# Queries and keys projected with the weights stationary and 512 tokens moving, keys turned back for their output, the decode's first cache fetches behind the queries' stores

## The chip, the cores and the metric

The kernel runs on one core of one Trainium2 chip. The metric is the device time of one execution in microseconds (us); the median of the runs shown is what two kernels are compared by. TensorE (PE) multiplies, and has a row of its own for weight loads (PEld); VectorE (DVE), ScalarE (ACT) and GpSimd (POOL) do the element-wise work; SyncE (SP) issues nearly all DMAs, on one queue. The granted clock of TensorE was 0.995 of full in the profiled execution.

## The reference

One layer of a streaming encoder runs on 1024 prompt tokens, and on 8 x 16 new tokens that are decoded against caches. RMSNorm is followed by one projection to queries, keys and values of two head groups. Group A (8 heads of 64) does stick-breaking attention over all the past; group B (8 heads) does softmax attention over a band of chunks. Then come per-head norms, an output projection, a gated feed-forward block and an input embedding.

```python
def trunk_layer(x, p, g_mix, w_in, ...):
    h = rmsnorm(x, g_mix)
    q_a, k_a, v_a, q_b, k_b, v_b = split_heads(h, w_in)      # h @ w_in, cut into six parts of 512 columns
    a = stick_breaking(q_a, k_a, v_a, ...)                   # prompt: causal; decode: the cache and the new frames
    o_b = chunk_band_prompt(q_b, k_b, v_b, rel_table)        # decode: band_attention over the cached band
    x = x + concat(rmsnorm(a), rmsnorm(o_b)) @ w_out
    x = x + (silu(rmsnorm(x) @ w_gate) * (rmsnorm(x) @ w_up)) @ w_down
    return x + sigmoid(rmsnorm(x) @ w_ple_gate) * (p @ w_ple_proj), (k_a, v_a, k_b, v_b)
```

The keys and values of the prompt (all rows of group A, the last 512 rows of group B) and of the decoded tokens are outputs too.

## The kernel before, in words

**Tokens and precision.** The 1024 prompt tokens and the 128 decoded ones make nine tiles of 128 tokens; the ninth is the decoded one. A product of float32 values is made of three matmuls of high and low parts (`mm3`, lines 105 to 108: high by high on line 106, and the two mixed ones on 107 and 108). The normalised activations are turned so that the contracted dimension lies on the partitions, and stay in SBUF as `hT`, in three groups of three token tiles (384 tokens, class `Transposed`).

**The projection.** `qkv` (line 217) is a generator which yields after each unit of TensorE work. It goes through twelve column groups of 256 columns of `w_in`, in the order of `loads` (line 289): keys of A (two groups), queries of A (two), values of A (two, interleaved), keys of B, values of B, queries of B. A column group's weights come by one DMA of 1 MB (`wraw`, a single buffer), and are split into high and low parts by ACT and POOL (lines 150 and 111).
- Keys and values (`others`, line 248): per token tile, 24 matmuls (8 slices of the contraction by 3) with the tokens as the stationary operand (lhsT) and 256 weight columns moving. The result `ps` holds tokens on partitions. ACT or DVE copies it to `st` (line 257), which is stored as the output (lines 278 and 284). Keys are also turned by TensorE (line 263, six transposes for three tiles), split into high and low parts (`parts`, lines 223 and 111) and stored to a DRAM scratch, `kT0h`, `kT0l` (group A) or `kT1h`, `kT1l` (group B).
- Queries (`queries`, line 234): per 128 columns and 384 tokens, 24 matmuls with the weights stationary and 384 tokens moving. The result is already turned; ACT and DVE scale and split it (lines 226 and 227) and it is stored to `qT0h`, `qT0l` and so on (line 232).

The high and low parts of one piece share one buffer `sq`, of which there are two; values use the same two buffers. A buffer is free again when its two stores have landed. The results `ps` have two PSUM banks, the transposes two (four in the first stage).

**What runs beside it.** A first stretch of the generator runs alone (lines 784 to 794: 36 units, to the sixth unit of the values of A). The next 30 units run beside the decode of group A, 1.2 decode steps for each unit (line 805, `R2`), with TensorE's order as written (`manual_schedule`). The decode reads the cache, 64 fetches of 512 KB into `draw` (line 135, seven buffers, six fetched ahead); it turns cached keys (line 395), makes scores (418), turns weights (404) and sums values (463). The last units run beside the prompt's attention, 1.95 attention steps for each (line 816): scores on lines 575 and 576, transposes on 608, sums over values on 631 and 632. Elsewhere a scheduler places each engine's instructions, with a model of their times; it also hoists the decode's first fetches on SP to where their buffers come free.

After that the attention goes on alone, from line 872 beside the decode of group B, whose first DMAs read the decoded tokens' queries and keys back from the scratch (line 355). Output projection, feed-forward and embedding follow; nothing in them is touched.

## Time and profile before

| | us |
|---|---|
| median of 3 runs | 1734.73 |
| lowest, highest | 1728.23, 1735.36 |
| the profiled execution's own time | 1727.71 |
| its span, first to last instruction | 1725.6 |
| PE busy in the span | 1668.2 |
| DVE, ACT, POOL busy | 1044.9, 776.4, 774.3 |

A row of a group of instructions gives the line, the engine, output and inputs by the program's names, partitions by elements, how often, the busy time and the mean duration of one in ns, and then the engine's idle time just before them with what ended it. TensorE's matmuls are pipelined: a duration of one overlaps the next, so what one matmul costs is read from the starts of many in a row.

### The profile page before, as it was taken

The page shows a single profiled execution, that of the slowest core. Times are in us where ns is not written, and L with a number is a line of the kernel's source. Part 1 is how long each engine was busy: PE and PEld are TensorE (multiplying, and loading weights), DVE is VectorE, ACT ScalarE, POOL GpSimd, SP SyncE. Part 2 cuts the span into 40 slices and gives each one's busy share as a digit, 9 for nine tenths or more (in the row PEclk, how much of TensorE's full clock was granted, in tenths as well). Part 3 has the DMA queues.
Part 4 walks back from the last instruction along what each step waited for, and adds up shares of the span by engine and source line. Part 5 has one row for each costly group of instructions (what it writes and reads, how often), then busy time and mean ns, then how long its engine had stood idle before and what let it go on. Part 6 is the DMA issues. An engine that isn't in the chain of part 4 may idle for free.

```text
span 1725.6 us, 29066 instructions
## 1 busy us (share of the span) xinstructions
PE 1668.2 (97%) x11076; PEld 1457.6 (84%) x11076; DVE 1044.9 (61%) x1640; ACT 776.4 (45%) x1698; POOL 774.3 (45%) x584
## 2 busy tenths in 40 slices
PE   8999999999997998899999999999999999999998
PEld 7998888889995887787778888888888788887998
DVE  5112344277778675654886666666666698887635
ACT  5214545276767776643643333333332343333432
POOL 2313301287446422222455555555554565558364
PEclk9999999999999999999999999999999999999999
DMA  5847898656469986855413222222222874311123
GB/s 191 278 145 226 287 293 284 189 171 184 119 176 267 296 252 185 232 165 176 142 56 115 88 87 90 95 95 95 95 95 95 291 292 136 120 39 61 59 71 141
DMA packets 172620, 279.40 MB, mean 162 GB/s; under 512 B 15297, under 2 KB 103617, under 8 KB 171074
## 3 DMA queue, kind: packets, MB, share of 16 engines
q1 hardware_dynamic: 172482, 277.55, 49.9%
q8 instruction: 88, 1.44, 0.4%
q14 instruction: 50, 0.41, 0.1%
HBM read 197.95 MB, written 79.56 MB: 161 GB/s over the span
## 4 chain that ended last, share of the span: by engine, by line
PE 86%; DMA 5%; DVE 3%; ACT 2%; issue 1%; POOL 1%; SPq 0%; POOLq 0%; ACTq 0%; DVEq 0%
PE ps L1056 20%; PE ps L106 9%; PE ps L107 9%; PE ps L108 9%; PE pt L1307 6%; PE ps L1307 4%; PE pt L1056 3%; PE pt L608 3%; PE pt L395 2%; PE po L632 2%; DMA mixn<-mixp 2%; PE acc L463 2%; PE po L631 2%; PE S L575 1%; PE sdec L418 1%; PE S L576 1%
## 5 line engine op out<-in xcount | busy, mean ns | idle before, releaser
L111 POOL TENSOR_TENSOR wlo<-wraw,whi 128x512 fp32r<-128x512 f32 (+1 forms) x127 | 224.4, 1794 | 205.6 <-ACT whi L150 201.7
L106 PE MATMUL ps<-whi,hTh 128*128 128x256 f32 x576 | 167.7, 291 | 0.1
L107 PE MATMUL ps<-wlo,hTh 128*128 128x256 f32 x576 | 164.2, 285 | 0.0
L108 PE MATMUL ps<-whi,hTl 128*128 128x256 f32 x576 | 163.9, 285 | 0.0
L150 ACT CAST whi<-wraw 128x512 fp32r<-128x512 f32 (+1 forms) x128 | 88.2, 753 | 94.1 <-PE ps L1056 64.8
L589 DVE TENSOR_TENSOR_SCAN keep<-keep,zero 128x128 f32<-128x128 f32 (+4 forms) x64 | 99.1, 1558 | 37.6 <-ACT keep L581 36.6
L590 POOL TENSOR_TENSOR w<-w,keep 128x127 f32<-128x127 f32 (+4 forms) x64 | 83.4, 1313 | 73.1 <-DVE keep L589 64.0
L106 PEld LDWEIGHTS ps<-whi,hTh 128*128 128x128 f32 x576 | 110.2, 191 | 6.0 <-issue 5.4
L108 PEld LDWEIGHTS ps<-whi,hTl 128*128 128x128 f32 x576 | 110.2, 191 | 0.5 <-DVE hTl L111 0.2
L107 PEld LDWEIGHTS ps<-wlo,hTh 128*128 128x128 f32 x576 | 110.3, 192 | 0.1
L111 DVE TENSOR_TENSOR wtl<-pt,wth 128x512 fp32r<-128x512 f32 (+1 forms) x192 | 94.2, 514 | 18.1 <-ACT wth L612 17.2
L612 ACT CAST wth<-pt 128x512 fp32r<-128x512 f32 (+1 forms) x192 | 84.4, 463 | 44.2 <-PE pt L608 43.4
L608 PE MATMUL pt<-ident,w 128*128 128x128 f32 x528 | 87.9, 278 | 5.5 <-POOL w L590 2.1
L106 PE MATMUL ps<-whi,hVh 128*128 128x256 f32 x288 | 81.9, 284 | 0.5 <-ACT hVh L1454 0.5
L107 PE MATMUL ps<-wlo,hVh 128*128 128x256 f32 x288 | 81.7, 284 | 0.0
L108 PE MATMUL ps<-whi,hVl 128*128 128x256 f32 x288 | 81.6, 284 | 0.0
L575 PE MATMUL S<-qk 128*128 128x384 f32 (+2 forms) x192 | 71.4, 373 | 5.8 <-ACT keep L581 3.9
L631 PE MATMUL po<-wth,vk 128*128 128x256 f32 (+1 forms) x304 | 76.3, 283 | 0.2
L608 PEld LDWEIGHTS pt<-ident,w 128*128 128x128 f32 x528 | 61.8, 141 | 15.4 <-issue 3.6
L632 PE MATMUL po<-wtl,vk 128*128 128x256 f32 (+1 forms) x304 | 72.7, 282 | 0.0
L111 POOL TENSOR_TENSOR actl<-actr,acth 128x1024 fp32r<-128x1024 f32 (+1 forms) x22 | 56.7, 2579 | 33.6 <-DMA sr<-acts 18.2
L106 PE MATMUL ps<-hTh,whi 128*128 128x384 f32 x192 | 66.0, 344 | 0.0
(359 smaller groups left out, 5335.9 us busy)
## 6 DMA issues: line engine op xcount, KB each, us to landing
draw<-in_cache_sb_k SPq DMA_DIRECT2D x32, 512.0 KB, 5.3
draw<-in_cache_sb_v SPq DMA_DIRECT2D x32, 512.0 KB, 5.1
act<-sg SPq DMA_DIRECT2D x11, 1152.0 KB
actr<-act SPq DMA_DIRECT2D x22, 576.0 KB, 5.4
wraw<-in_w_in SPq DMA_DIRECT2D x11, 1024.0 KB, 5.2
wraw<-in_w_gate SPq DMA_DIRECT2D x11, 1024.0 KB
wraw<-in_w_up SPq DMA_DIRECT2D x11, 1024.0 KB
v<-sv SPq DMA_DIRECT2D x36, 256.0 KB, 4.5
```

What stands on the lines that cost most here:

```text
L106: T.matmul(out, lhsT=ah, rhs=bh, start=start, stop=False)
L107: T.matmul(out, lhsT=ah, rhs=bl, start=False, stop=False)
L108: T.matmul(out, lhsT=al, rhs=bh, start=False, stop=stop)
L111: eng.tensor_tensor(out, a, hi.bitcast(F32), op=ALU.subtract)
L150: A.copy(h[:, o], v[:, o])
L575: T.matmul(sc, lhsT=hd["qq"][:, qs], rhs=hd["kkh"][:, kc], start=True, stop=False)
L589: V.tensor_tensor_scan(rev, rev, zero[:, 0:1].to_broadcast([P, n]), 1.0, op0=ALU.mult, op1=ALU.add)
L608: T.transpose(pt[:, (c - c0) * P : (c - c0 + 1) * P], w[:, c * P : (c + 1) * P], ident)
L631: T.matmul(dst, lhsT=vs, rhs=wth[:, kb - base, c0:c1], start=(i == 0), stop=False)
L632: T.matmul(dst, lhsT=vs, rhs=wtl[:, kb - base, c0:c1], start=False, stop=(i == nkb - 1))
L1056: T.matmul(out, lhsT=a[x][:, k], rhs=b[y][:, k], start=(not more and k == 0 and n == 0), stop=(k == 3 and n == 2), skip_group_check=more)
L1307: T.matmul(out, lhsT=a[i][:, x, m * P : (m + 1) * P], rhs=b[j][:, x], start=(not more and x == 0 and n == 0), stop=(x == 1 and n == 2), sk ...
```

## The change

Keys and queries now go through one function, `columns`: 512 tokens move past stationary weights of 128 columns, twice, for each of the two halves of a column group (24 matmuls each, with a yield after 12 of them). The ninth token tile is done apart (`last_tile`, tokens stationary as in `rows_of`, 256 columns moving, two transposes). `hT` becomes two halves of 512 tokens and a tile for the decoded tokens (class `Halves`). The eviction to the scratch goes in two pieces of 256 columns, each in one `sq` buffer with two stores. Where the keys are an output, ACT or DVE copies the result to a new tile `u`, TensorE turns it back with four transposes, the other of the two engines copies that to `kn`, and it is stored. For queries of B the ninth tile comes first. The first column group keeps `others`, because the token tiles are still being made beside it.

The decode's first fetches are pinned behind a store (`issue_after`), the eighth store of the second query group of A. The counts follow the new units: 42 units before the decode (36 before), 30 up to the attention as before, of which 29 now have decode steps beside them at 1.2 each, and 1.625 attention steps for each of the 36 last units (1.95 for 30 before; 58.5 both times).

```diff
--- before.py
+++ after.py
@@ -179,6 +179,27 @@
             g, o = divmod(t, 3)
             return [self.t[n][g][half][:, :, o * P : (o + 1) * P] for n in range(2)]
 
+    class Halves:
+
+
+        def __init__(self, pool):
+            self.b = [[[pool.tile([P, 4, 512], F32R, name=f"hT{k}{n}{x}") for x in "hl"] for k in range(2)]
+                      for n in range(2)]
+            self.last = [pool.tile([P, KT, P], F32R, name="hT8" + x) for x in "hl"]
+
+        def rows(self, n, k):
+            return [v[:, k % 4] for v in self.b[n][k // 4]]
+
+        def tok(self, t, k):
+            if t == NP:
+                return [v[:, k] for v in self.last]
+            return [v[:, (t % 4) * P : (t % 4 + 1) * P] for v in self.rows(t // 4, k)]
+
+        def dst(self, t, half):
+            if t == NP:
+                return [v[:, half * 4 : half * 4 + 4] for v in self.last]
+            return [v[:, :, (t % 4) * P : (t % 4 + 1) * P] for v in self.b[t // 4][half]]
+
     def transposed(pst, h, hT, t):
 
         for half in range(2):
@@ -214,7 +235,9 @@
     kv_prompt = {(0, 1): sb_k_p, (0, 2): sb_v_p, (1, 1): cb_k_p, (1, 2): cb_v_p}
     kv_sample = {(0, 1): sb_k_s, (0, 2): sb_v_s, (1, 1): cb_k_s, (1, 2): cb_v_s}
 
-    def qkv(ch, hT, stg, first, second):
+    stores = []
+
+    def qkv(ch, hT, stg, keyp, first, second):
 
         def parts(n, src, scale=1.0):
             both = stg.tile([P, 2, 384], F32R, name="sq", tag="sq")
@@ -227,33 +250,75 @@
                 V.scalar_tensor_tensor(hl[1], src, scale, hl[0].bitcast(F32), op0=ALU.mult, op1=ALU.subtract)
             return [x.bitcast(F32) for x in hl]
 
-        def transposed_out(grp, w, c, g, hl):
+        def parts_out(grp, w, c, lo, n, src):
+
+            hl = parts(n, src, (1.0, (1 - 2 * grp) * HD**-0.5)[w == 0])
             for x in range(2):
-                nc.sync.dma_start(qkT[grp][w][x][c, :, g * 384 : (g + 1) * 384], hl[x])
-
-        def queries(grp, c, wts):
-            wh, wl = wts
-
-            order = [(pr, g) for pr in range(2) for g in range(3)]
-            if (grp, c) == (1, 1):
-                order.sort(key=lambda x: x[1])
-            for pr, g in order:
-                m = slice(pr * P, (pr + 1) * P)
-                ps_ = ps["o"].tile([P, 384], F32, name="ps", tag="O")
-                for k in range(KT):
-                    mm3(ps_, wh[:, k, m], wl[:, k, m], *hT.rows(g, k), k == 0, k == KT - 1)
-                transposed_out(grp, 0, c * 2 + pr, g, parts(384, ps_, (1 - 2 * grp) * HD**-0.5))
-                yield
+                stores.append(nc.sync.dma_start(qkT[grp][w][x][c, :, lo : lo + n], hl[x]))
+
+        def rows_of(t, wts):
+
+            ps_ = ps["o"].tile([P, 256], F32, name="ps", tag="O")
+            for k in range(KT):
+                mm3(ps_, *hT.tok(t, k), wts[0][:, k], wts[1][:, k], k == 0, k == KT - 1)
+            return ps_
+
+        def last_tile(grp, w, c, wts):
+
+            st = stg.tile([P, 3, 256], F32, name="st", tag="st", bufs=2)[:, 0]
+            A.copy(st, rows_of(NP, wts))
+            if w:
+                nc.sync.dma_start(kv_sample[grp, w][0, :, :, c * 4 : c * 4 + 4, :].rearrange("b i h d -> (b i) (h d)"), st)
+            yield
+            pt = ps["t"].tile([P, 256], F32, name="pt", tag="T")
+            for pr in range(2):
+                T.transpose(pt[:, pr * P : (pr + 1) * P], st[:, pr * P : (pr + 1) * P], ident)
+            hl = parts(256, pt, (1.0, (1 - 2 * grp) * HD**-0.5)[w == 0])
+            for x in range(2):
+                nc.sync.dma_start(qkT[grp][w][x][c * 2 : c * 2 + 2, :, NP * P :].rearrange("c p n -> p c n"),
+                                  hl[x].rearrange("p (c n) -> p c n", c=2))
+
+        def columns(grp, w, c, wts):
+
+            last = last_tile(grp, w, c, wts)
+            if w == 0 and grp:
+
+                last = iter(())
+                yield from last_tile(grp, w, c, wts)
+            for n in range(2):
+                for pr in range(2):
+                    m = slice(pr * P, (pr + 1) * P)
+                    ps_ = ps["o"].tile([P, 512], F32, name="ps", tag="O")
+                    for k in range(KT):
+                        mm3(ps_, wts[0][:, k, m], wts[1][:, k, m], *hT.rows(n, k), k == 0, k == KT - 1)
+                        if k == 3:
+                            yield
+                    kept_ = w and (n or not grp)
+                    if kept_:
+                        u = keyp["p"].tile([P, 512], F32, name="u", tag="u", bufs=3)
+                        (V.tensor_copy if pr else A.copy)(u, ps_)
+                    for o in (0, 256):
+                        parts_out(grp, w, c * 2 + pr, n * 512 + o, 256, ps_[:, o : o + 256])
+                    yield
+                    if kept_:
+                        pt = ps["t"].tile([P, 512], F32, name="pt", tag="T")
+                        for t in range(4):
+                            T.transpose(pt[:, t * P : (t + 1) * P], u[:, t * P : (t + 1) * P], ident)
+                        st = keyp["p"].tile([P, 512], F32, name="kn", tag="kn", bufs=3)
+                        (A.copy if pr else V.tensor_copy)(st, pt)
+                        first_row = n * 512 - grp * 512
+                        nc.sync.dma_start(
+                            kv_prompt[grp, w][0, 0, first_row : first_row + 512, c * 4 + pr * 2 : c * 4 + pr * 2 + 2, :]
+                            .rearrange("(t p) h d -> p t (h d)", p=P),
+                            st.rearrange("p (t m) -> p t m", t=4))
+            yield from last
 
         def others(grp, w, c, wts, gs):
 
-            wh, wl = wts
             for g in gs:
                 st = stg.tile([P, 3, 256], F32, name="st", tag="st", bufs=2)
                 for o in range(3):
-                    ps_ = ps["o"].tile([P, 256], F32, name="ps", tag="O")
-                    for k in range(KT):
-                        mm3(ps_, *hT.tok(g * 3 + o, k), wh[:, k], wl[:, k], k == 0, k == KT - 1)
+                    ps_ = rows_of(g * 3 + o, wts)
                     (V.tensor_copy if o % 2 else A.copy)(st[:, o], ps_)
                     yield
                 if w == 1:
@@ -261,7 +326,7 @@
                         pt = ps["t"].tile([P, 384], F32, name="pt", tag="T")
                         for o in range(3):
                             T.transpose(pt[:, o * P : (o + 1) * P], st[:, o, pr * P : (pr + 1) * P], ident)
-                        transposed_out(grp, 1, c * 2 + pr, g, parts(384, pt))
+                        parts_out(grp, 1, c * 2 + pr, g * 384, 384, pt)
                 else:
                     for o in range(3):
                         sv = stg.tile([P, 2, 384], F32R, name="sv", tag="sq").rearrange("p a b -> p (a b)")[:, :512]
@@ -307,9 +372,9 @@
                     yield
                 continue
             load(i + 1)
-            if w == 0:
-                yield from queries(grp, c, wts)
-            elif (grp, w) != (0, 2):
+            if w < 2:
+                yield from columns(grp, w, c, wts)
+            elif grp:
                 yield from others(grp, w, c, wts, range(3))
             elif c == 0:
 
@@ -747,10 +812,7 @@
     first, start = ExitStack(), ExitStack()
     banks(right, "right", o=2)
     banks(start, "left", t=4, g=1)
-    hT = Transposed()
-    for g in range(3):
-        for half in range(2):
-            hT.add(hp, half, "hT", (g,))
+    hT = Halves(hp)
     all_engines = {getattr(mybir.EngineType, e) for e in ("PE", "Activation", "DVE", "Pool", "SP")}
     with tc.tile_pool(name="x1", bufs=2, side="right") as xp, tc.manual_schedule(engines=all_engines):
 
@@ -781,7 +843,8 @@
             sub(V if i == 3 else G, w_first[1][:, o], w0[:, o], w_first[0][:, o])
         transposed(ps["t"], rows.pop(0), hT, 0)
         rows += [row(1), row(2)]
-        project = qkv(ch, hT, stg, w_first, ch.raw(cols(w_in[0], 3), KT, 256))
+        keyp, kstack = {}, ExitStack()
+        project = qkv(ch, hT, stg, keyp, w_first, ch.raw(cols(w_in[0], 3), KT, 256))
         next(project)
         transposed(ps["t"], rows.pop(0), hT, 1)
         for t in range(2, NT):
@@ -790,8 +853,9 @@
             transposed(ps["t"], rows.pop(0), hT, t)
             next(project)
     start.close()
+    keyp["p"] = pool(kstack, "keys", "right")
     banks(first, "left", t=2, s=1)
-    advance(project, None, 0, 36 - (NT - 1))
+    advance(project, None, 0, 42 - (NT - 1))
 
     for i, g in enumerate((g_out_sb, g_out_cb)):
         nc.sync.dma_start(g_out[:, i * 4 : i * 4 + 4], g.rearrange("o (k p) -> p (o k)", p=P))
@@ -801,19 +865,24 @@
     banks(dstack, "right", d=2, a=1)
     dp = pool(first, "dA", "left")
     dec = decode(0, Chunks(dp, "d", 1024, RAWS, 2), dp)
+    behind = stores[-9].ins
+    advance(project, None, 0, 1)
+    with tc.issue_after(behind):
+        next(dec)
     with tc.manual_schedule(engines={mybir.EngineType.PE}):
-        advance(project, dec, R2, 30)
+        advance(project, dec, R2, 29)
         for _ in dec:
             pass
     first.close()
     dstack.close()
+    kstack.close()
 
 
     banks(left, "left", s=2, t=4)
     at = pool(left, "at", "left")
     run, pairs, done = attention(at, ps, LAG)
     att = run(range(8))
-    advance(project, att, 1.95)
+    advance(project, att, 1.625)
     right.close()
 
 
```

## The prediction

> **What bounds the kernel now.** I read the page first, then the busy times by stage, then TensorE's rows in order of time, and the DMAs of the stages that change.
>
> ```profile
> span 1725.6 us, 29066 instructions
> PE 1668.2 (97%) x11076; PEld 1457.6 (84%) x11076; DVE 1044.9 (61%) x1640; ACT 776.4 (45%) x1698; POOL 774.3 (45%) x584
> PE 86%; DMA 5%; DVE 3%; ACT 2%; issue 1%; POOL 1%; SPq 0%; POOLq 0%; ACTq 0%; DVEq 0%
> ```
>
> TensorE is busy for 97% of the span and carries 86% of the chain that ended last. The change works in the first 515 us, so the stages there decide.
>
> ```profile
> core 0: us, PE busy (x) PEld busy (x) DVE busy (x) ACT busy (x) POOL busy (x), PEclk, DMA share, GB/s
> 0.00:152.00 152.00, 144.38 (x1032) 139.88 (x1032) 41.60 (x76) 53.34 (x105) 41.85 (x43) 1.00 0.61 205
> 152.00:325.00 173.00, 171.45 (x1969) 150.66 (x1969) 66.58 (x100) 81.21 (x215) 35.50 (x42) 1.00 0.81 261
> 325.00:515.00 190.00, 186.23 (x1374) 175.23 (x1373) 133.76 (x164) 127.16 (x314) 111.82 (x85) 1.00 0.61 172
> 515.00:550.00 35.00, 26.31 (x198) 21.11 (x197) 31.28 (x43) 26.05 (x67) 26.11 (x19) 0.99 1.01 295
> ...
> 340.00:366.00 26.00, 22.24 (x172) 20.23 (x171) 14.36 (x16) 15.63 (x40) 22.05 (x14) 1.00 0.69 194
> ```
>
> To 152 us the projection runs alone, to 325 beside the decode of group A, to 515 beside the attention. TensorE is idle for 1.6 us of 173 and 3.8 of 190 (all of it between 340 and 366). So in these stages a matmul saved is time saved, as long as nothing else comes late. Next is the decode stage's DMA with a share of 0.81. Behind 515, with the projection gone, DVE works for 31.3 of 35 us.
>
> A busy TensorE says nothing of what one matmul costs, since durations overlap. I take it from the first and the last start of an unbroken run: values before the decode (183 rows), queries (123 rows), and a stretch of the feed-forward with 512 columns moving (84 rows).
>
> ```profile
> 127.79 0.28 PE L106 MATMUL ps<-whi,hTh 128*128 128x256 f32 x1
> 149.93 0.28 PE L108 MATMUL ps<-whi,hTl 128*128 128x256 f32 x1
> 83.76 0.33 PE L106 MATMUL ps<-hTh,whi 128*128 128x384 f32 x1
> 104.90 0.33 PE L108 MATMUL ps<-hTh,wlo 128*128 128x384 f32 x1
> 1119.00 0.40 PE L1056 MATMUL pt<-T2h,S1h 128*128 128x512 f32 x1
> 1137.84 0.39 PE L1056 MATMUL ps<-B11h,wlo 128*128 128x512 f32 x1
> 288.96 1.04 PE L395 MATMUL pt<-ident,draw 128*128 128x128 f32 x8
> 289.83 0.38 PE L404 MATMUL pt<-ident,wdec 128*128 128x128 f32 x2
> ```
>
> 22.14 us by 182 steps is 121.6 ns for 256 columns; 21.14 by 122 is 173.3 ns for 384; 18.84 by 83 is 227.0 ns for 512; eight transposes in 0.87 us are 109 ns each. Each step of 128 columns costs 52 to 54 ns, so some 14 to 16 ns belong to the matmul itself, and this is all that fewer and longer matmuls can save.
>
> **The change part by part.** *Matmuls.* A column group of keys had 9 x 24 matmuls of 256: 216 x 0.1216 = 26.27 us. Now it has 4 x 24 of 512 and 24 of 256: 96 x 0.2270 + 24 x 0.1216 = 24.71. Three groups change (the first keeps its form): 3 x -1.56 = -4.7 us. A group of queries had 144 of 384, 24.95 us, and has 24.71: 4 x -0.24 = -1.0 us. *Transposes.* Keys of A as before, 18. Keys of B: 10 for 18, as only rows that are outputs are turned back; queries: two more in each of four groups. Together 8 fewer, -0.9 us. The sum is -6.6 us of TensorE.
>
> The price for 512 comes from another stage, but its form is the same (stationary 128 x 128, moving 512, float32) and that stage has no idle time either. [...]
>
> *Evictions.* The shapes of after stand in neighbouring rows.
>
> ```profile
> L257 ACT COPY st<-ps 128x256 f32<-128x256 f32 x48 | 18.0, 376 | 74.6 <-PE ps L108 74.6
> L396 ACT COPY kT<-pt 128x512 f32<-128x512 f32 x32 | 18.7, 585 | 27.7 <-PE pt L395 19.9 <-issue 6.5 <-ACT keep L425 0.7
> L396 DVE COPY kT<-pt 128x512 f32<-128x512 f32 x32 | 22.1, 689 | 49.5 <-PE pt L395 45.6 <-ACT sv L270 3.9
> L111 DVE TENSOR_TENSOR wtl<-pt,wth 128x256 fp32r<-128x256 f32 x13 | 5.4, 413 | 2.3 <-ACT wth L612 2.3
> ```
>
> A key unit of 24 x 0.227 = 5.45 us asks ACT for 0.59 + 2 x 0.38 = 1.3 us and DVE for 0.69 + 2 x 0.41 = 1.5. Both have room in the first two stages (53 and 42 of 152 us, 81 and 67 of 173), so I cost them at nothing; without that cover 1.5 us would show in each of the 8 units that keep their keys, 12 us. The turning back comes later than its unit, so TensorE should not wait for the copy `u`. TensorE in the second key group of A, before, where a group of three tiles ends (`ps` tokens by columns, `hTh` and `hTl` the activations, `st` the copied result):
>
> ```order
> L106 MATMUL ps<-whi,hTh_148 128x256
> L107 MATMUL ps<-wlo,hTh_148 128x256
> L108 MATMUL ps<-whi,hTl_149 128x256
> L263 MATMUL pt<-ident,st 128x128 x4
> L106 MATMUL ps<-whi,hTh_138 128x256
> ```
>
> And now, in the same column group (`hT10h`: second half of the contraction, first 512 tokens, high part):
>
> ```order
> L106 MATMUL ps<-hT10h,whi 128x512
> L107 MATMUL ps<-hT10l,whi 128x512
> L108 MATMUL ps<-hT10h,wlo 128x512
> L306 MATMUL pt<-ident,u 128x128 x4
> L106 MATMUL ps<-hT01h,whi 128x512
> L107 MATMUL ps<-hT01l,whi 128x512
> L108 MATMUL ps<-hT01h,wlo 128x512
> ```
>
> The operands have changed places, and a unit's four transposes stand a whole unit (24 matmuls) behind it, since its successor's last matmul comes first.
>
> *Stores.* This is the place I trust least. A unit of queries took 24 x 0.173 = 4.2 us and one `sq` buffer; now 5.45 us and two, and there are only two. So a buffer must come round in 5.45 us instead of 8.3: ACT 0.38, DVE 0.41, two issues of 0.32 each, and the landing. It holds while a store lands within 4.0 us.
>
> ```profile
> L232 SPq DMA_DIRECT2D qT0h<-sq x12: 320/320/332, 84.9 to 129.9; - x12
> ...
> qT0h<-sq SPq DMA_DIRECT2D x12, 192.0 KB, 2.3
> qT0l<-sq SPq DMA_DIRECT2D x12, 192.0 KB, 1.9
> kT0h<-sq SPq DMA_DIRECT2D x8, 192.0 KB, 3.9
> ...
> draw<-in_cache_sb_k SPq DMA_DIRECT2D x1, 512.0 KB, 9.1
> ...
> kT1h<-sq SPq DMA_DIRECT2D x10, 192.0 KB, 4.8
> kT1l<-sq SPq DMA_DIRECT2D x10, 192.0 KB, 5.1
> ```
>
> Queries' stores landed in 1.9 to 2.3 us, keys' stores beside the cache fetches in 3.9, in the decode stage in 4.8 to 5.1. The last two don't matter there, since decode steps stretch a unit to about 10 us. In the first stage I take 2.3, with no wait; for the range I take 5.1, a cycle of 6.6 us.
>
> *The first fetches.* SP before: they stand among the keys' stores of the first group (`out` from `st` is the keys' output).
>
> ```order
> L278 DMA out<-st 128x3x256
> L135 DMA draw<-in_cache_sb_k 128x2x512 x4
> L278 DMA out<-st 128x2x256
> L135 DMA draw<-in_cache_sb_k 128x2x512 x2
> L341 DMA odd<-in_consts 128x2
> ```
>
> Now they stand behind the second unit of the last query group:
>
> ```order
> L257 DMA qT0h<-sq 128x256
> L257 DMA qT0l<-sq 128x256
> L135 DMA draw<-in_cache_sb_k 128x2x512 x6
> L406 DMA odd<-in_consts 128x2
> L257 DMA qT0h<-sq 128x256
> L257 DMA qT0l<-sq 128x256
> ```
>
> So the fetches wait for that unit's last store, and have moved past the second key group's stores, 26 stores of queries and four weight loads. Behind them on SP and in the DMA queue now stand the stores of two units and of the last tile. Six fetches are 3.1 MB, by this row of 52 to 150 us some 8 us.
>
> ```profile
> GB/s 393 385 377 370 393 125 252 296 374 338 59 0 245 268 289 353 58 190 102 157 3 15 170 221 366 144 161 0 161 90 70 7 161 232 199 316 340 55 277 164
> ```
>
> The next stores are issued 5.45 us later, so they find 3 us of it still ahead; one unit may be evicted a us late, and the second `ps` bank covers that. The data is wanted by the decode near 150 us and lands near 125, so the delay costs nothing; without that cover it would be the 9.1 us of one late fetch.
>
> *Decode and pacing.* One decode step fewer stands beside the projection (34 for 35, as the first call now only sets up). The values of B fill TensorE there as before, so I cost it at nothing. The attention gets 1.625 steps a unit: as many in all.
>
> *The sum:* 0 for evictions, stores and pacing, -6.6 us of TensorE. Against the profiled execution this is 1727.7 - 6.6 = 1721.1. That execution and the three runs lie at 1728 and at 1735, two each; their middle is 1731.5, the median of the three runs 1734.7. I forecast from the middle: 1731.5 - 6.6 = 1725 us, of its own 1719 to 1731.
>
> **The rivals.** *A, the stores become the bound (slower).* In the first stage 12 units change. If the landing is 5.1 us, each waits 1.1 us: +13 - 6.6 = +7, 1738 us. It decides from a landing of 4.0 us on; at 4.6 us nothing would be gained, and at the 9.1 of the late fetch it would be 12 x 5.1 - 6.6 = +54. For it: smaller pieces, twice as many on one queue, and ACT has waited for such a store already.
>
> ```profile
> ACT sq L226 <- DMA qT0l<-sq: 5.6, 1, 5.6
> ```
>
> [...] Against it: the fetches are gone from the first 10, where 2.3 us was enough. Chance 0.12.
>
> *B, the decode stage is paced by its DMA.* Its share is 0.81 at 261 GB/s. If the cache sets the pace, the two key groups of B gain nothing there, and -6.6 loses 2 x 1.56 + 1.7 = 4.9: 1730 us. Against it: 1.6 us of idle time on TensorE in 173. Chance 0.15.
>
> *C, the idle time beside the attention goes too (faster).* The 3.8 us between 340 and 366 lie where POOL works 22 of 26 us; 1.625 steps for 1.95 lighten it. And the decode of B gets its queries earlier, where two of the 8.7 idle us behind 515 may go. -6.6 - 3.8 - 2 = -12.4: 1719 us. Against it: the number of attention steps is the same, so DVE and POOL may only be late elsewhere. Chance 0.23.
>
> **How the numbers follow.** The forecast has the remaining 0.50. A measurement of this kernel can tell some 0.5%, 8.7 us, from no change. Faster by more: C, and a sixth of the forecast's own (its lower end): 0.31. Slower by more: A with a landing from 5.3 us, and a little for what I have not seen: 0.10. Within it: 0.59. The range goes from below C, 1715, to A, 1738.
>
> **What would show it.**
>
> ```profile
> 150.77 1.03 PE L395 MATMUL pt<-ident,draw 128*128 128x128 f32 x8
> ...
> 320.12 1.08 PE L463 MATMUL acc<-draw,wt 128*32 128x128 f32 x32
> ```
>
> Right: starts 227 ns apart in the key and query rows of 512 columns; the decode's first transposes 1.6 us earlier than 150.8 (one key group, two query groups, four transposes more), its last sums 6.5 us earlier than 320.1 (two key groups and 16 transposes on top). Wrong: ACT or DVE waiting for DMAs of `sq` and TensorE for `ps` before 150 us (A); TensorE waiting on `draw` (B); the same idle time behind 340 us, or less (C).

## The result and the profile after

| | before | changed |
|---|---|---|
| median, us | 1732.41 (22 runs, 1724.99 to 1735.72) | 1735.73 (22 runs, 1732.23 to 1738.98) |
| ratio | | 1.0025, interval 1.0017 to 1.0033 |
| profiled execution, us (span) | 1727.71 (1725.6) | 1738.54 (1736.7) |

The change makes the kernel about a quarter of a percent slower: 3.3 us by the medians, 4.3 by the ratio. That lies within the 0.5% and within the range, but the 6.6 us of the forecast are gone, and more: some 11 us have to be found.

The two profiled executions differ by 10.8 us, which is too much: the first lies at the low end of before's runs, the second at the high end of the changed kernel's. So I set the changed kernel against a second profile of before (span 1731.4, the first experiment below). The page of the changed kernel, with the busy times of the engines and the chain that ended last:

```profile
PE 1677.3 (97%) x10684; PEld 1435.3 (83%) x10684; DVE 1055.0 (61%) x1660; ACT 777.7 (45%) x1716; POOL 777.3 (45%) x584
PE 83%; DMA 6%; DVE 3%; ACT 3%; POOL 2%; issue 1%; SPq 1%; POOLq 0%; ACTq 0%; DVEq 0%
```

TensorE has 392 instructions fewer (384 matmuls and 8 transposes), and 83% of the chain for 86%. Its busy time by stage, in the same windows as before the change:

```profile
0.00:152.00 152.00, 143.13 (x885) 126.89 (x886) 45.20 (x84) 55.07 (x112) 40.89 (x42) 1.00 0.62 203
152.00:325.00 173.00, 170.10 (x1781) 140.37 (x1780) 70.98 (x107) 80.93 (x219) 39.09 (x45) 1.00 0.81 265
325.00:515.00 190.00, 182.65 (x1274) 163.22 (x1273) 130.04 (x162) 121.97 (x305) 109.73 (x80) 0.98 0.59 164
340.00:366.00 26.00, 21.95 (x152) 20.61 (x152) 13.01 (x15) 15.08 (x38) 18.91 (x13) 0.87 0.43 133
```

Beside the attention TensorE is idle for 7.35 us of 190 (3.77 and 3.23 in the two profiles of before), and between 340 and 366 us its granted clock has fallen to 0.87. When certain matmuls start tells where the time goes. The changed kernel: first transposes of the decode, its last sums, the attention's first scores, first and last sums of outputs.

```profile
151.94 1.04 PE L460 MATMUL pt<-ident,draw 128*128 128x128 f32 x8
319.20 1.08 PE L528 MATMUL acc<-draw,wt 128*32 128x128 f32 x32
332.17 0.47 PE L640 MATMUL S<-qk 128*128 128x128 f32 x2 [0.32 <-DMA qk<-kT0h]
352.53 0.37 PE L696 MATMUL po<-wth,vk 128*128 128x256 f32 x1
799.87 0.28 PE L697 MATMUL po<-wtl,vk 128*128 128x128 f32 x1
```

The same five in the second profile of before:

```profile
151.01 1.04 PE L395 MATMUL pt<-ident,draw 128*128 128x128 f32 x8
320.36 1.08 PE L463 MATMUL acc<-draw,wt 128*32 128x128 f32 x32
332.31 0.40 PE L575 MATMUL S<-qk 128*128 128x128 f32 x2
343.13 0.37 PE L631 MATMUL po<-wth,vk 128*128 128x256 f32 x1
795.48 0.28 PE L632 MATMUL po<-wtl,vk 128*128 128x128 f32 x1
```

| changed minus before, us | predicted | measured | lost since the row above |
|---|---|---|---|
| decode's first transposes | -1.6 | +0.9 | 2.5 |
| decode's last sums | -6.5 | -1.2 | 2.8 |
| attention's first scores | -6.5 | -0.1 | 1.0 |
| attention's first output sums | -6.5 | +9.4 | 9.5 |
| attention's last output sums | -6.6 | +4.4 | -5.0 (given back) |

So there are three losses: 2.5 us before 152, 2.8 us beside the decode, and some 5.5 us around the attention's start.

*Before 152 us.* SP's queue, with the fetches (`draw`) and the query stores around them:

```profile
116.21 3.33 SPq L135 DMA_DIRECT2D draw<-in_cache_sb_k  x6
...
120.42 0.38 SPq L257 DMA_DIRECT2D qT0h<-sq  x1
...
123.30 0.32 SPq L257 DMA_DIRECT2D qT0l<-sq  x1
```

ACT a little later; the bracket gives the idle time before a row and who ended it. `sv` (a value tile's parts) shares its two buffers with `sq`:

```profile
136.30 0.41 ACT L335 CAST sv<-st 128x256 fp32r<-128x256 f32 x1 [2.39 <-DMA qT0l<-sq]
...
142.48 0.40 ACT L335 CAST sv<-st 128x256 fp32r<-128x256 f32 x1 [5.32 <-DMA v<-sv]
```

What TensorE waits for between 50 and 152 us (line waited for; total, times, longest):

```profile
PE ps L106 <- ACT st L322: 1.8, 2, 1.1
```

ACT waits for these stores, behind it the copies `st` that free the banks of `ps` come late, and TensorE waits for them. That is the chain of rival A, in its last two units, and it ends in the shorter of the two waits (0.7 us, at 143.21). The longer one (1.1 us, at 130.73) has a load in it and not a store: a small table, `causal`, is loaded behind the fetches, and DVE's copy of it stands ahead of DVE's parts of the last query unit:

```profile
128.90 0.77 DVE L411 TENSOR_SCALAR causalb<-causal 128x16 bf16<-128x16 f32 x1 [9.60 <-DMA causal<-in_consts]
```

ACT's next part waits 1.6 us for DVE (to 130.03), and the copy `st` comes behind it. Another 0.5 us of TensorE's idle time, at 126.27, is the wait of the last tile's transposes for their own copy.

*At the attention's start.* ACT in the changed kernel, then in the second profile of before. A `wth` makes the part that the first output sums need:

```profile
339.80 0.27 ACT L677 CAST wth<-pt 128x128 fp32r<-128x128 f32 x1
344.29 0.40 ACT L335 CAST sv<-st 128x256 fp32r<-128x256 f32 x1 [4.22 <-DMA v<-sv]
344.60 0.37 ACT L677 CAST wth<-pt 128x256 fp32r<-128x256 f32 x1
```

```profile
339.59 0.69 ACT L612 CAST wth<-pt 128x128 fp32r<-128x128 f32 x2
344.88 0.40 ACT L270 CAST sv<-st 128x256 fp32r<-128x256 f32 x1 [4.60 <-DMA v<-sv]
```

Both kernels have the wait for a value store. Before, both `wth` stood ahead of it; now it stands between them, and the second is 4.2 us late. The store stands behind the second head's loads on SP, and the first head's loads behind a key store (that `kT1h` is the last tile's, turned at the end of its column group):

```profile
322.54 0.59 SPq L546 DMA_DIRECT2D mixs<-ow  x1
324.25 0.37 SPq L278 DMA_DIRECT2D kT1h<-sq  x1
325.05 0.52 SPq L591 DMA_DIRECT2D qk<-qT0h  x1
...
329.97 0.91 SPq L591 DMA_DIRECT2D qk<-qT0h  x1
...
334.66 2.15 SPq L338 DMA_DIRECT2D v<-sv  x2
```

TensorE stands still until a copy of DVE frees a bank:

```profile
346.07 0.58 PE L106 MATMUL ps<-whi,hT8h 128*128 128x256 f32 x1 [3.63 <-DVE st L322]
```

On DVE that copy stands behind `wtl`, which waits for the second `wth`, and waits a little more for POOL's part of the value tile; both follow ACT's wait for the value store. In the second profile of before TensorE pauses behind that store too (ACT's `keep` comes right behind the waiting `sv`), but for 2.3 us, and with its first output sums done:

```profile
346.11 0.50 PE L575 MATMUL S<-qk 128*128 128x512 f32 x1 [2.32 <-ACT keep L581]
```

The next windows give the clock (the last column but two) from 0.7 us ahead of the end of the changed kernel's pause on, and in and behind the pause of before:

```profile
345.40:352.20 6.80, 6.13 (x27) 5.85 (x28) 2.89 (x4) 3.30 (x9) 3.91 (x5) 0.50 0.46 163
```

```profile
343.50:346.10 2.60, 0.29 (x3) 0.15 (x2) 0.00 (x0) 1.22 (x4) 0.68 (x1) 1.00 1.11 346
347.20:350.60 3.40, 3.40 (x18) 3.40 (x18) 2.56 (x4) 3.06 (x9) 2.95 (x3) 0.50 0.50 177
```

### The profile page after: what moved, and what is told of

Its sections match the earlier page's. It is cut to its first block, busy times and chain, and to the rows that moved or that the text cites. A ratio compares the mean times of both kernels' runs of the same rounds, so it can differ in the third digit from the quotient of the medians.

```text
span 1736.7 us, 28465 instructions
## 1 busy us (share of the span) xinstructions
PE 1677.3 (97%) x10684; PEld 1435.3 (83%) x10684; DVE 1055.0 (61%) x1660; ACT 777.7 (45%) x1716; POOL 777.3 (45%) x584
## 4 chain that ended last, share of the span: by engine, by line
PE 83%; DMA 6%; DVE 3%; ACT 3%; POOL 2%; issue 1%; SPq 1%; POOLq 0%; ACTq 0%; DVEq 0%
PE ps L1125 20%; PE ps L106 9%; PE ps L107 8%; PE ps L108 8%; PE pt L1376 6%; PE ps L1376 4%; PE pt L1125 3%; PE pt L673 2%; PE pt L460 2%; PE po L697 2%; PE po L696 1%; PE acc L528 1%; PE S L640 1%; PE sdec L483 1%; DMA v<-sv 1%; PE S L641 1%
## 5 line engine op out<-in xcount | busy, mean ns | idle before, releaser
L640 PE MATMUL S<-qk 128*128 128x384 f32 (+2 forms) x192 | 73.5, 385 | 3.1 <-ACT keep L646 1.9
L641 PE MATMUL S<-qk 128*128 128x384 f32 (+2 forms) x192 | 64.3, 337 | 0.3 <-DMA qk<-kT0l 0.3
L461 DVE COPY kT<-pt 128x512 f32<-128x512 f32 x48 | 33.0, 688 | 49.8 <-PE pt L460 45.8
L1376 PE MATMUL pt<-wlo,acth 128*128 128x512 f32 x160 | 62.4, 390 | 0.3 <-DVE wlo L111 0.3
L1376 PE MATMUL pt<-whi,actl 128*128 128x512 f32 x160 | 62.2, 389 | 0.0
L111 POOL TENSOR_TENSOR S1l<-s,S1h 128x512 fp32r<-128x512 f32 x21 | 27.3, 1302 | 76.3 <-ACT S1h L1155 76.3
L1381 DVE TENSOR_TENSOR x<-x,ps 128x512 f32<-128x512 f32 x70 | 46.9, 680 | 23.3 <-PE ps L108 13.2
L696 PEld LDWEIGHTS po<-wth,vk 128*128 128x128 f32 x304 | 59.0, 194 | 2.5 <-DVE wtl L111 0.7
```

The costliest lines, as they stand in the source:

```text
L111: eng.tensor_tensor(out, a, hi.bitcast(F32), op=ALU.subtract)
L640: T.matmul(sc, lhsT=hd["qq"][:, qs], rhs=hd["kkh"][:, kc], start=True, stop=False)
L696: T.matmul(dst, lhsT=vs, rhs=wth[:, kb - base, c0:c1], start=(i == 0), stop=False)
L1376: T.matmul(out, lhsT=a[i][:, x, m * P : (m + 1) * P], rhs=b[j][:, x], start=(not more and x == 0 and n == 0), stop=(x == 1 and n == 2), sk ...
```

## The experiments

Theories, as the expectations number them: (1) query stores behind the moved fetches; (2) the pause at the attention's start and the half clock behind it; (3) the price of 512 columns beside the decode; (4) the pace; (5) a value store behind the second head's loads. Ratios are to the kernel before on the same chip; 0.001 is 1.7 us.

**e0, the kernel before once more.**

> The kernel before, unchanged, for a second profile and the granted clock of each of its runs. The changed kernel had 0.986 to 0.993. If the clock carries the difference (theory 2 below), most runs here show 0.993 to 0.997; if the 0.995 of the first profile was one lucky run, they lie at 0.986 to 0.993 as well. Its idle time behind 340 us should be 2.5 us again, under the 3.8 us of the changed kernel. Theories for the group: (1) the query stores and the first value stores come late, hold the two sq buffers and so TensorE (2.8 us before 152 us); (2) a pause of 3.8 us at the attention's start is answered by half clock (345 to 352 us, some 3.4 us); (3) a matmul of 512 beside the decode costs 240 ns and not 227, so the saving was never there (2.5 us).

Measured: 1730.11 us, ratio 0.9990 (0.998 to 1.000): an unchanged kernel comes out 0.1% off, so no more than that can be told. The span of its profile is 1731.4 us, its clock 0.990 (0.995 in the first profile), and the half clock behind the attention's start is there in before as well, half as long (3.4 us for 6.8). So part of the 10.8 us between the first two profiles goes with the clock (two executions of before on one chip, of 1724.91 and 1735.83 us, had 0.997 and 0.990), and so does part of what a pause costs (behind it the clock was 0.50 for 3.4 us here, and 1.00 in the first profile); half clock as such is not the change's own.

**e1 and h1, three buffers.** The first trial cut the first key group's pieces of 384 in two:

```diff
-            both = stg.tile([P, 2, 384], F32R, name="sq", tag="sq")
+            both = stg.tile([P, 2, 256], F32R, name="sq", tag="sq", bufs=3)
...
-                        parts_out(grp, 1, c * 2 + pr, g * 384, 384, pt)
+                        for o, n in ((0, 256), (256, 128)):
+                            parts_out(grp, 1, c * 2 + pr, g * 384 + o, n, pt[:, o : o + n])
```

> The changed kernel with three sq buffers of 256 columns for two of 384 (the same bytes; the first key group writes its 384 columns as 256 and 128). Theory 1: the stalls at 125, 129 and 142 us go, the decode's first transposes come 2.8 us earlier (149.2 for 151.9), and the first values' copies find a buffer at 327 us, so that the pause at 342 us shrinks too: 1735.7 - 2.8 - 2 to 4 = 1729 to 1731. Theory 2: what is gained before 152 us is gained only if the pause at 342 us falls under that of before; if it stays at 3.8 us, the time is 1733. Theory 3: no more than 1 us.

Measured: 1743.54 us, 1.0058 (1.0043 to 1.0073). A miss of the experiment: the added pieces delay the start (TensorE waits 1.8 us for ACT's copies of the activations near 50 us, and the first transposes come at 158.3). By its time it tells nothing of the buffers. The second trial leaves those pieces whole, in buffers of their own:

```diff
+            both = (wide["p"] if n > 256 else stg).tile([P, 2, max(n, 256)], F32R, name="sq", tag="sq", bufs=2 if n > 256 else 3)
...
+    advance(project, None, 0, 2)
+    wstack.close()
```

> The changed kernel with three sq buffers of 256 columns, and the first key group's pieces of 384 in two buffers of their own that are given back before the second group's keys (the first trial of three buffers cut these pieces in two, which cost 6 us ahead of 152 us). The order on TensorE ahead of the decode is unchanged. Theory 1: the stalls at 129 and 142 us go (2.2 of 2.8 us), the first transposes come at 149.8 for 151.9: 1735.7 - 2 = 1733.5. Theory 5 adds: with a third buffer the value copies wait less at 334 and 344 us, up to -3 more: 1730 to 1731. If neither holds: 1735 to 1737.

Measured: 1733.40 us, 1.0019 (1.0009 to 1.0030); the first transposes at 149.55, no wait for `ps` left, with the fetches where the changed kernel has them. By these rows theory 1 holds in the first stage; the time is not clear of the changed kernel's. At the attention's start nothing is gained: the first output sums come at 344.8, but the pause is now at 357 us, 3.9 us for POOL's `w`.

**e2, the fetches behind all query stores.** `ends` collects the last tile's stores.

```diff
-    behind = stores[-9].ins
+    behind = ends[-1].ins
```

> The changed kernel with the decode's first six cache fetches pinned behind the last tile's stores of the last query group instead of behind its second unit. Theory 1: no query store stands behind the fetches any more, the stalls before 152 us fall from 2.8 to under 1 us and the first transposes come some 2 us earlier; the fetches are issued some 17 us later (133 for 116), so their data lands near 143, which still covers 149: 1733 to 1734. If the stalls stay, the queue of the two sq buffers alone is slow and the moved fetches are innocent. Theories 2 and 3: 1735 to 1736, as nothing behind 320 us changes.

Measured: 1732.90 us, 1.0003 (0.9995 to 1.0012), so 3.8 us less than the changed kernel. The window from 100 to 149 us (TensorE's busy time is the second number), first of the changed kernel, then of this one with the start of its first transposes:

```profile
100.00:149.00 49.00, 46.69 (x300) 42.23 (x299) 5.77 (x13) 12.51 (x29) 14.43 (x10) 1.00 0.73 235
```

```profile
100.00:149.00 49.00, 49.00 (x325) 45.16 (x325) 5.38 (x14) 12.63 (x29) 13.66 (x9) 1.00 0.63 205
```

```profile
149.19 1.03 PE L460 MATMUL pt<-ident,draw 128*128 128x128 f32 x8
```

All of TensorE's idle time is gone, and the transposes come 1.8 us earlier than in before: the 1.6 us of the prediction. What stands behind the fetches made the stalls, which is theory 1 with the load of `causal` beside the stores: DVE's copy of that table now comes at 144.67, behind all query parts. Two buffers suffice where no fetch stands ahead.

**e3, the fetches where before has them.** The move alone undone.

```diff
-    with tc.issue_after(behind):
-        next(dec)
+    next(dec)
```

> The changed kernel with its one edit on the fetches undone: the first six cache fetches stand among the first key group's stores again, as in the kernel before. Theory 1: the stalls before 152 us (2.8 us and more) were these fetches ahead of the query stores, and go; the first transposes come at 149.4, the time falls by 2.5 to 4 as with the fetches behind all stores (1732.9): 1732 to 1733, ratio 1.001. If the stalls stay, the fetches are innocent and two sq buffers are too few for the new pieces in themselves. If new stalls come up with the keys' stores of the first groups, the move was needed: 1736 or more.

Measured: 1739.36 us, 1.0046 (1.0033 to 1.0060). Its windows, and what TensorE waits for:

```profile
50.00:100.00 50.00, 45.27 (x213) 37.50 (x212) 9.42 (x21) 12.56 (x25) 9.41 (x4) 0.97 0.74 236
100.00:149.00 49.00, 49.00 (x307) 44.34 (x306) 6.65 (x16) 12.23 (x28) 12.25 (x7) 1.00 0.49 152
```

```profile
PE ps L106 <- DVE sq L111: 4.4, 1, 4.4
```

The stalls from 100 us on go, so the fetches made them; but ahead of the second key group the fetches cost 4.4 us in one piece. There, too, a load is in the chain: ACT waits for the next weights, which are loaded behind the fetches, and the second unit's parts, on ACT and then on DVE, stand behind that:

```profile
61.71 1.99 ACT L150 CAST whi<-wraw 128x1024 fp32r<-128x1024 f32 x2 [4.99 <-DMA wraw<-in_w_in]
```

Before, ACT waits 3.2 us for the same weights and TensorE not at all. So of the three places tried, the new form bears the 3.1 MB only behind all query stores; whether the stores would have been late as well at the early place is not shown.

**e4, the attention's loads behind the keys' last stores.**

```diff
+    advance(project, None, 0, 1)
+    with tc.issue_after(ends[-1].ins):
+        run, pairs, done = attention(at, ps, LAG)
...
-    advance(project, att, 1.625)
+    advance(project, att, 1.67)
```

> The changed kernel with one projection step drawn ahead of the attention and the attention's first loads of qk issued behind the last tile's key stores, which stood behind six of those loads (1.67 attention steps a unit, for the one unit that is gone). Theory 2: ACT no longer waits 7.8 us for kT1l from sq, the values' stores are ahead of the second head's loads, the pause at 342 us falls below 2 us and with it goes the half clock behind it: -2 to -7, 1729 to 1734. Theory 1, in its part before 152 us: nothing changes, the stalls stay at 2.8 us; theory 3: nothing changes. A miss would be a pause that only moves to the attention's first scores, since they may start 0.5 to 1 us later.

Measured: 1739.00 us, 1.0033 (1.0021 to 1.0045). Theory 2 falls in this form: ACT waits 3.4 us for the key store, but then 6.7 us for a value store, which still stands behind both heads' loads, and the pause is 4.5 us, before the scores. It is the value store that matters, which made theory 5.

**e6, the queries alone in the new form.**

```diff
-            if w < 2:
+            if w == 0:
                 yield from columns(grp, w, c, wts)
-            elif grp:
+            elif (grp, w) != (0, 2):
                 yield from others(grp, w, c, wts, range(3))
```

> The changed kernel with the keys of all groups in the old form (216 matmuls of 256 and the transposes ahead of the stores, no turning back); the queries, the fetches and the pace as in the changed kernel. By the rows, the keys' new form gave 1.6 us in the first stage (the second key group) and some 2 us beside the decode: without it 1735.7 + 1.6 + 2 + the decode's own waits of the new form given back (-1.5) = 1738. If the new form of the keys is what costs (its copies, its turning back, the half units between decode steps), this one is faster than the changed kernel: 1733 or less. The stalls of the query stores before 152 us (2.7 us) stay in either case.

Measured: 1740.06 us, 1.0056 (1.0042 to 1.0069), 5.4 us more than the changed kernel. So the keys' new form is a gain, 2.3 us of it beside the decode (169.6 us from the first transposes to the last sums, 167.3 in the changed kernel), and the loss comes with the queries and fetches: here one stall from 130 us on is 3.5 us long, again with `causal` in its chain (DVE waits 10.2 us for it), and that stall is part of the 5.4.

**f1, f2, f4, the pace.** On the changed kernel, on e2, and mirrored on before (1.625 and 2.4375):

```diff
-    advance(project, att, 1.625)
+    advance(project, att, 1.95, 18)
+    advance(project, att, 1.3)
```

> The changed kernel with the attention paced as before: 1.95 steps behind each of the 18 value units, 1.3 behind each of the 18 query half units (58.5 in all, as with 1.625 throughout). Theory 4 (pace): with 29 instead of 35 steps beside the values, TensorE pauses for 7.8 us between the attention's start and the queries (3.7 in the second profile of before), and the attention with the projection leaves 6 pairs of scores and 12 sums of outputs for later; so here -4 us: 1731 to 1732, a ratio to before of 1.000, the pauses at 367 and 377 us gone. If the start pause at 342 us and the clock alone make the loss, the pace changes nothing: 1735 to 1737. A miss the other way: more steps beside the values meet the same late value stores, and the pauses grow.

Measured: 1748.00 us, 1.0094 (1.0076 to 1.0111).

> The changed kernel with both: the first cache fetches behind all query stores (that alone measured 1732.9) and the attention paced as before. If theories 1 and 4 both hold and add: 1732.9 - 4 = 1729, a ratio of 0.998 to before, and first scores at 330.4 us again. If the pace is innocent: 1733.

Measured: 1739.89 us, 1.0062 (1.0042 to 1.0082).

> The kernel before with its attention spread evenly over TensorE's time as in the changed one: 1.625 steps behind each of 18 value units and 2.4375 behind each of 12 query units (58.5 as before). Nothing else differs. Theory 4: 3 to 4 us slower than before, with new pauses between 345 and 410 us and the first query unit about 4 us later than 409. If the pace is innocent: the time of before within 1 us.

Measured: 1731.69 us, 1.0007 (0.9995 to 1.0018). Theory 4 falls on both sides: the even pace costs before nothing, and the old pace would cost the changed kernel 12 us more. Its pauses at 367 and 377 us stay, and TensorE is busy for 58.4 us of the 63 from 417 to 480, for 62.3 in the changed kernel. Why the old pace is that bad with half units was not followed up.

**g1 and g3, the second head's loads later,** on the changed kernel and on before.

```diff
                         if hh == 0:
-                            head(st[pr], 1)
+                            if pr:
+                                head(st[pr], 1)
...
+                    elif (pr, hh, t) == (0, 0, 4):
+                        head(st[0], 1)
```

> The changed kernel with the second head's six loads of qk called for at the fifth attention step instead of the second, so that the first value store beside the attention is issued ahead of them. In the changed kernel ACT has a value copy (sv) between its first two copies wth, and waits there 4.2 us for that store, which stands behind those loads; TensorE pauses 3.8 us at 342 us and the first sums of outputs (po) come at 352.5 for 343.1. Theory 5 (a store behind loads, at the attention's start): the store lands some 5 us earlier, the pause falls under 1.5 us, the first po comes before 348, and the time falls by 3 to 4: 1732, ratio 1.000. If the pause only moves to the second head's scores (late loads) or the loss lies elsewhere: 1735 to 1737.

Measured: 1734.02 us, 1.0011 (0.9999 to 1.0024), 2.4 us less than the changed kernel; the two intervals overlap, so the rows say more than the time. SP and ACT:

```profile
333.20 0.85 SPq L338 DMA_DIRECT2D v<-sv  x1
334.10 0.45 SPq L591 DMA_DIRECT2D qk<-qT0h  x1
```

```profile
340.24 0.41 ACT L335 CAST sv<-st 128x256 fp32r<-128x256 f32 x1 [0.69 <-DMA v<-sv]
...
346.43 0.41 ACT L335 CAST sv<-st 128x256 fp32r<-128x256 f32 x1 [2.66 <-DMA v<-sv]
```

The store is ahead of the second head's loads, and the first output sums come 13.4 us behind the first scores (335.8 to 349.2), 20.4 in the changed kernel, 10.8 in before. From the first scores to the last output sums it is 463.1 us, as in before (463.2), for 467.7. (In this profile TensorE stood idle for 4.0 us between 100 and 152 us, where the changed kernel has 2.3.)

> The same edit on the kernel before, as a control: before, both copies wth stand ahead of the waiting sv on ACT, and the pause is 2.5 us. Theory 5: at most the pause goes, -2 us and a ratio of 0.999; so the edit is worth less here than on the changed kernel. If it is worth as much as there (-3 or more), the loss at the attention's start is not the change's.

Measured: 1730.24 us, 1.0001 (0.9990 to 1.0013). But here the edit does not do what it did in g1. SP issues the second head's loads from 331.40 to 335.95 us, and the value stores still behind them:

```profile
336.05 2.50 SPq L273 DMA_DIRECT2D v<-sv  x2
```

The pause stays, at 2.4 us. So this run is no control, and what an earlier store would give the kernel before is open. That the loss at the attention's start is the changed kernel's rests on the rows of the two kernels (467.7 us for 463.2); that the late store makes it (theory 5) rests on g1, and on g2 below.

**g2 and g4, both cures; h2.** g2 is e2 and g1 together, g4 is e3 and g1, h2 is e2 and h1.

> The changed kernel with both cures: the first fetches behind all query stores (alone a ratio of 1.0003) and the second head's loads called for at the fifth attention step (alone 1.0011; the changed kernel 1.0025). If the two losses are separate, the cures add: 1.0025 - 0.0022 - 0.0014 = 0.999, some 1729, with first scores at 330.4 us, no pause over 2 us behind them, and the attention's end 2 us ahead of that of before. If they share one cause (clock, or the loads' bandwidth), the sum stays at 1.0003 or above.

Measured: 1728.39 us, 0.9986 (0.9975 to 0.9998). Within the intervals the cures add: 3.8 and 2.4 us alone, 6.8 together. Three of the five starts, the third 463.2 us behind the second as in before:

```profile
148.95 1.04 PE L460 MATMUL pt<-ident,draw 128*128 128x128 f32 x8
...
329.07 0.47 PE L640 MATMUL S<-qk 128*128 128x128 f32 x2 [0.20 <-DMA qk<-kT0h]
...
792.28 0.28 PE L697 MATMUL po<-wtl,vk 128*128 128x128 f32 x1
```

This is 0.4% faster than the changed kernel. Against before it is 0.14%, where an unchanged kernel came out at 0.10%: level or a little faster. Since before never had its value store earlier (g3), this does not compare the two forms at their best.

> The same with the fetches where the kernel before has them instead of behind the query stores, and the second head's loads at the fifth step. If where the fetches go does not matter as long as no query store is behind them: as the last, 0.999. If the early place costs the first groups' stores something: 1.000 to 1.002.

Measured: 1737.00 us, 1.0037 (1.0026 to 1.0049): the early place costs here as in e3.

> The changed kernel with both cures of theory 1: the first cache fetches behind all query stores (alone 1732.9) and the three sq buffers of 256 columns. The first cure leaves no stall before 152 us, so the buffers can give nothing more there: 1732.9 by theory 1 alone. What is gained beyond that is gained at the attention's start (theory 5): up to -3, 1730.

Measured: 1735.24 us, 1.0030 (1.0019 to 1.0042), worse than e2 alone. The third buffer has nothing left to cure in the first stage, and at the attention's start the pause is again 3.9 us for POOL's `w`: it lets the value tiles in earlier, not the attention. Its time is not clear of h1's.

## Why the prediction was wrong

*Stores and fetches: the step that failed.* The prediction let the next stores "find 3 us of it still ahead", one unit a microsecond late, covered by the second bank, and costed the move at 0. Two units and the last tile stood behind the fetches with two buffers for their stores, and it cost 2.5 us by the start rows and 3.8 by e2. ACT's first part of the last unit came at 128.06 us, where e2 has it at 123.31: 4.8 us late, and not one. And the prediction asked only about stores: the small load of `causal` behind the fetches made the longer of the two stalls. Rival A had the late stores, and by its own count of 10 units without the fetches also their place, the last 2 of 12; but its price was worked out for all 12, and its 0.12 was kept for that. In the other ten units TensorE never waited, as the prediction said.

*Matmuls: right in kind, too large.* Beside the decode, a unit of 24 values of 256 in the first profile of before, its first two rows and what follows the last:

```profile
233.36 0.39 PE L106 MATMUL ps<-whi,hTh 128*128 128x256 f32 x1
233.58 0.28 PE L107 MATMUL ps<-wlo,hTh 128*128 128x256 f32 x1
...
236.33 1.03 PE L395 MATMUL pt<-ident,draw 128*128 128x128 f32 x8
```

And a half unit of 12 keys of 512 in the changed kernel, the first two rows and what follows the last:

```profile
231.80 0.50 PE L106 MATMUL ps<-hT01h,whi 128*128 128x512 f32 x1
232.14 0.40 PE L107 MATMUL ps<-hT01l,whi 128*128 128x512 f32 x1
...
234.70 1.03 PE L460 MATMUL pt<-ident,draw 128*128 128x128 f32 x8
```

2.97 us became 2.90, where 24 x 0.1216 - 12 x 0.227 = 0.19 us were forecast. The 16 half units of the stage take 2.84 to 2.91 us, 2.88 in the mean: together 1.5 us saved, for 3.1. The first matmul behind other work takes 220 ns before and 340 now, some 100 ns more than the next ones in both, so the starts cancel. What is left lies in the steps: my 121.6 ns held one break (0.35 us from 130.18 to the next start at 130.53) and is 120 without it, and a step of 512 columns is 229 to 233 ns here, not 227; why it is longer here than in the feed-forward stays open. TensorE is also idle for 2.9 us of the stage, for 1.6 and 1.8 in the profiles of before. So by the start rows the stage is 2.1 us shorter, for 4.9; e6 gives 2.3 for the keys' form.

*Evictions* at nothing: nearly right; TensorE waits once for the copy `u`.

```profile
306.39 0.66 PE L306 MATMUL pt<-ident,u 128*128 128x128 f32 x4 [0.81 <-DVE u L299]
```

*Pacing* at nothing: right, as far as f4 shows it on before. But the prediction took the attention's start as given. With other units ahead of it, ACT's order there changed: the wait for a value store, which in before comes behind both copies `wth` and costs a pause of 2.3 us, fell between the two. The pause is 3.6 us, and the half clock that comes with it 6.8 us for 3.4; in it the matmuls of 256 columns start 214 ns apart (346.44 to 349.86 us, 16 steps), behind it 118 (353.20 to 353.91, 6 steps). With the store earlier, 4.6 of the 5.5 us are back by the rows of g1, 2.4 by its time; no step spoke of it. Rival C had the idle time beside the attention go; it doubled. Rival B is out: TensorE is busy for 170.1 of 173 us, and the cache is not what it waits for.

*What would show it:* the decode's transposes and sums failed both marks, by 2.5 and 5.3 us, and the waits named for A were there. With both cures (g2) the kernel is 2.4 us below before, 4.2 short of the forecast; 2.8 of these are lost beside the decode, which takes 167.3 us in g2 as in the changed kernel.

What stays open: the 1.0 us by which the first head's loads wait for a key store (325.05 for the 323.1 at which SP was free) was not tried alone. What an earlier value store would give the kernel before is not known. g1 changes the orders on ACT and TensorE along with the store, so these two causes were not parted. And the half clock that comes with a pause varies between executions: 3.4 us of it in the second profile of before, none in the first.

## What to carry to other kernels

When a large transfer is moved on a queue, count everything behind it, not only the next store: every store until the buffers have all come round, and every small load that an engine waits for ahead of other work (here two units, the last tile and `causal`: 2.5 us by the start rows). Of the three places tried here, the one behind the last of the stores cost nothing (in e2 TensorE was busy for all 49.00 us from 100 to 149). When matmuls are saved ahead of a stage, look at the order that the scheduler then writes at the stage's start: a wait that stood behind two instructions of the critical chain may now stand between them (here the second `wth` came 4.2 us late). A price per matmul has to be taken from rows of the stage it is used for (512 columns: 227 ns in the feed-forward, 229 to 233 beside the decode). An edit that is to be a control has to move the same instructions there; its trace shows whether it does.

## What the runs showed of the hardware

The granted clock was 0.50 from 347.2 to 350.6 us (3.4 us) in the second profile of before, 1.1 us behind the end of a pause of 2.3 us, and from 345.4 to 352.2 us (6.8 us) in the changed kernel, from 0.7 us ahead of the end of a pause of 3.6 us. In the first profile of before the same pause of 2.3 us (to 346.09) has no half clock with it: 1.00 from 340 to 366 us.

In the two units shown above, the first matmul behind other work cost some 100 ns more than the next ones, at 256 columns (220 for 120 ns, 233.36 to the next start at 233.58) as at 512 (340 for 233 ns).

A value store issued at 334.66 behind thirteen loads of 0.25 MB and more freed its buffer at 344.3, 9.6 us later; ahead of the second six (g1) it was issued at 333.20 and freed it at 340.2, 7.0 us later.
